# Linear ReLU attention: ten output stores moved from SyncE's queue into the loads' queue on GpSimd

## The chip, the cores and the metric

The kernel runs on one core of one Trainium2 chip. The metric is the time of one execution on the device in microseconds; lower is better. Three runs of the kernel before took 127.21, 126.92 and 126.89 us, median 126.92 us. Engines are named as in the profile: PE is TensorE, DVE is VectorE, ACT is ScalarE, POOL is GpSimd, SP is SyncE.

## The reference: attention without a softmax

```python
def reference(Q, K, V):                      # each (8, 12, 512, 64) float32
    Q_feat = np.maximum(0, Q)
    K_feat = np.maximum(0, K)
    KV = np.einsum('bhkd,bhkv->bhdv', K_feat, V)
    K_sum = np.sum(K_feat, axis=2)
    numerator = np.einsum('bhqd,bhdv->bhqv', Q_feat, KV)
    denominator = np.einsum('bhqd,bhd->bhq', Q_feat, K_sum)
    return numerator / (denominator[:, :, :, None] + 1e-10)
```

There are 96 heads of 512 rows and 64 columns. For each head a 64x64 matrix KV and a sum over K's rows are made from K and V; then every row of Q is multiplied by KV and divided by its product with that sum. Q, K and V are 12.58 MB each and so is the output: 37.75 MB are read from HBM and 12.58 MB are written to it.

## The kernel before, in words

**Tiles.** Eight heads make an octet; there are `NO` = 12 octets, 0 to 11. The heads' rows lie one after the other in HBM, so an octet is a block of 1 MB in each of Q, K, V and the output, seen as 128 partitions of 8 KB. Four heads make a group `g`; octet `o` has the groups `2*o` and `2*o + 1`. K and V are loaded by group (0.5 MB of float32 in HBM each), Q by octet (1 MB). The loads turn float32 into bfloat16 on the way, so what they write to SBUF is half of what they read: the profile counts the bytes written, and 210 GB/s of a load are 420 GB/s read from HBM. The output is float32 on both sides.

**Loads.** All loads but the first two are issued by POOL, in one queue (q0 in the profile): `load_kv` (lines 97 to 101) issues K and V of a group, `load_q` (103 to 105) Q of an octet. After `load_q(0)` a loop at line 115 issues, for each octet 1 to 11, K, V, K, V, Q: 3 MB read from HBM in five DMAs. The loop stands ahead of everything else in POOL's program; what holds an issue back is that its buffer must be free (12 buffers each for K and V, 7 for Q) and that the DMA eight places earlier in the queue must have landed, since POOL's DMAs go round eight completion semaphores. K and V of octet 0 come as float32 through the queues of SP and ACT (lines 111 and 112).

**Compute.** For each octet: `prep` and `prep_v` (DVE, ACT) apply the ReLU to K and lay K and V out for two heads at a time; `mm_kv` (PE, line 187) adds up KV and K's sums in PSUM; `evac_kv` copies them to SBUF; `qt` (lines 218 to 220) transposes Q on PE and applies the ReLU; `denom` makes the divisors and their reciprocals; `out_t` multiplies; `back` transposes the result back on PE; `norm` (line 271, DVE) divides and writes `o_sb`, twice for each octet, and then the octet's 1 MB is ready to be stored. The order on each engine is the program's order, which is written out by hand in the loops from line 321 on: the compute of octet `o` runs ahead of `backs(o - 1)`, which calls `norm` and `store`.

**Stores.** `store` (lines 277 to 287) issues one DMA of 1 MB on SP for octets 0 to 10, in a hardware queue (q1), and two of 0.5 MB for octet 11. The output tiles have `DELAY + 2` = 7 buffers. Ahead of the stores of octets 0 to 6 SP issues a small copy out of `k_sb` of octet `o + DELAY` into `scratch` (2 to 14 rows of 128 bytes, `PROBE`). This copy must wait until that K tile has landed, and since SP works through its program in order, the store behind it waits too: store 0 goes out when the first K tile of octet 5 has landed, and store 6 when that of octet 11 has. Stores 7 to 11 have no such copy, and go out when their octet is ready and SP has come to them.

Of the kernel before, what the change touches and what calls it, by code (L numbers as in the profile page):

```python
# [10 lines left out]
def kernel(  # L11
# [7 lines left out]
    nc = tc.nc  # L19
    B, H, S, D = Q.shape  # L20
# [11 lines left out]
    NO = NG // 2  # L32
    assert NO * 8 == NH and R == 16 and RQ == 32
    DELAY = 5
    PROBE = (8, 12, 4, 2, 14, 10, 6)

    fp32 = mybir.dt.float32
    bf16 = mybir.dt.bfloat16
# [3 lines left out]
    def pool(name, bufs, **kw):  # L42
        return ctx.enter_context(tc.tile_pool(name=name, bufs=bufs, **kw))

    consts = pool("consts", 1)
# [35 lines left out]
    mask = consts.tile([P, 2, 2], fp32, name="mask")  # L81
    mask8 = consts.tile([P, 4], fp32, name="mask8")
    mask8k = consts.tile([P, 2], fp32, name="mask8k")
    scratch = consts.tile([16, D], bf16, name="scratch")

    mask_h = consts.tile([P, 8, 2], fp32, name="mask_h")

# [7 lines left out]
    q_sb, k_sb, v_sb = {}, {}, {}  # L95

    def load_kv(g):
        k_sb[g] = kin.tile([P, R, D], bf16, name="k_sb")
        nc.gpsimd.dma_start(out=k_sb[g].rearrange("p r d -> p (r d)"), in_=Kr[g], single_packet=True)  # L99
        v_sb[g] = vin.tile([P, R, D], bf16, name="v_sb")  # L100
        nc.gpsimd.dma_start(out=v_sb[g].rearrange("p r d -> p (r d)"), in_=Vr[g], single_packet=True)  # L101

    def load_q(o):
        q_sb[o] = qin.tile([P, U, 2 * D], bf16, name="q_sb")
        nc.gpsimd.dma_start(out=q_sb[o].rearrange("p u f -> p (u f)"), in_=Qr[o], single_packet=True)  # L105
# [6 lines left out]
    nc.scalar.dma_start(out=v8.rearrange("p r d -> p (r d)"), in_=V8[0])  # L112
    load_q(0)
    make_identity(nc, ident)
    for o in range(1, NO):
        load_kv(2 * o)
        load_kv(2 * o + 1)
        load_q(o)

    def zero_masks():  # L120
        for h in range(NHG):
            for s in range(2):
                nc.vector.memset(mask[32 * h:32 * h + 32, 0, s:s + 1], 1.0 if h % 2 == s else 0.0)
        for t in range(2):
            nc.vector.memset(mask[:, 1, t:t + 1], 0.0)
            nc.vector.memset(mask[64 * t:64 * t + 64, 1, t:t + 1], 1.0)
# [148 lines left out]


    def store(o, o_sb):
        if o + DELAY < NO:
            n = PROBE[o]
            nc.sync.dma_start(out=scratch[0:n], in_=k_sb[2 * (o + DELAY)][0:n, 0, :])  # L280
        Ov = Or[o].rearrange("p (r d) -> p r d", d=D)
        if o == NO - 1:
            for j in range(2):
                rs = slice(RQ // 2 * j, RQ // 2 * (j + 1))
                nc.sync.dma_start(out=Ov[:, rs], in_=o_sb[:, rs])
            return
        nc.sync.dma_start(out=Ov, in_=o_sb)

    def out_tile():
        return outp.tile([P, RQ, D], fp32, name="o_sb", tag="o_sb")  # L290
# [17 lines left out]
    def backs(o):  # L308
        o_sb = out_tile()
        for j in range(2):  # L310
            norm(o, j, back(o, j), o_sb)
        store(o, o_sb)
# [26 lines left out]
    o = NO - 2  # L339
# [10 lines left out]
    o_sb = out_tile()  # L350
# [4 lines left out]
    for i in range(2):  # L355
        relu_q(o + 1, i, transp(o + 1, i), nc.vector if i == 1 else None)
    norm(o, 1, ps, o_sb)
    store(o, o_sb)
    idle(5, o + 1)
    out_t(o + 1, (0,))  # L360
# [32 lines left out]
```

## Time and profile before

| what | us |
|---|---|
| median of three runs | 126.92 |
| span of the profiled execution, first to last instruction | 125.2 |
| PE, DVE, ACT, POOL busy | 84.8, 83.4, 80.8, 32.4 |
| time of the packets of q0 (POOL's loads), as a share of 16 DMA engines' span | 74.4% |
| the same of q1 (SP: all stores, K of octet 0, the small copies) | 27.0% |

The profile gives the span of the execution that it recorded and no other time for it. The median stands 1.7 us above that span; this is what lies around the span (start and end of the program, and the difference between executions), and it is carried along unchanged below. Times inside the span are counted from its first instruction. "POOL" lines are work of GpSimd's cores, among them the writing of a DMA's descriptors; "SPq" lines are SyncE's sequencer, issuing or waiting.

### The profile page before, as it was taken

The numbers are of one execution on the slowest core, as the hardware profiler recorded it, in microseconds if no ns is written. First come the engines' busy times: TensorE is split into PE (matmuls) and PEld (weight loads), VectorE is DVE, ScalarE is ACT, GpSimd is POOL, SyncE is SP. The second block draws the span as 40 slices with busy tenths as digits, with TensorE's granted clock in tenths as the row PEclk, the third lists the DMA queues.
The fourth block names the chain that finished last, engine by engine and source line by source line (L and its number), as shares of the span: only waits on it lengthen the run. The fifth ranks groups of instructions, "written<-read, shape, count | busy, mean of one in ns | idle before, by whom it ended". The sixth has DMA issues, their size and how long they took to land.

```text
span 125.2 us, 2668 instructions
## 1 busy us (share of the span) xinstructions
PE 84.8 (68%) x1067; PEld 76.4 (61%) x1067; DVE 83.4 (67%) x192; ACT 80.8 (65%) x112; POOL 32.4 (26%) x62
## 2 busy tenths in 40 slices
PE   0005768497989898893598596199867767797800
PEld 0005548487978787791597494199766566696600
DVE  2719727979797998789148759433946936988440
ACT  0008989789898989988348688164929828637300
POOL 6903624415344241232133124034022000000000
PEclk9999999999999999999959999657999999999997
DMA  3999999999999999999999999999999999999993
GB/s 84 387 321 209 210 210 210 216 206 220 204 215 208 208 220 316 261 214 286 297 214 274 310 213 253 332 209 218 347 234 215 326 256 215 324 416 432 419 393 141
DMA packets 10348, 32.68 MB, mean 261 GB/s; under 512 B 1248, under 2 KB 1248, under 8 KB 8672
## 3 DMA queue, kind: packets, MB, share of 16 engines
q0 software_dynamic: 8064, 17.83, 74.4%
q1 hardware_dynamic: 2128, 13.64, 27.0%
q10 hardware_dynamic: 144, 1.05, 2.1%
q8 instruction: 8, 0.13, 0.4%
q14 instruction: 4, 0.03, 0.1%
HBM read 37.75 MB, written 12.58 MB: 402 GB/s over the span
## 4 chain that ended last, share of the span: by engine, by line
DMA 56%; PE 17%; DVE 15%; POOL 3%; issue 2%; ACT 1%; DVEq 1%; POOLq 0%
DMA q_sb<-in_Q_dram 25%; DMA v_sb<-in_V_dram 19%; DMA k_sb<-in_K_dram 12%; PE ps_kv L187 9%; DVE o_sb L271 8%; PE ps_bk L265 4%; PE ps_qt L208 4%; DVE kf L173 2%; DVE vo_all L175 1%; DVE vo_all L182 1%; DVEq L388 1%; POOL q_sb L105 1%; POOL v_sb L101 1%; POOL k_sb L99 1%; ACT ot_sb L240 1%
## 5 line engine op out<-in xcount | busy, mean ns | idle before, releaser
L271 DVE TENSOR_TENSOR o_sb<-ps_bk,rec 128x1024 f32<-128x1024 f32 x24 | 28.3, 1218 | 14.5 <-PE ps_bk L265 14.5
L187 PE MATMUL ps_kv<-vo_all,kf 128*128 128x132 bf16 x352 | 26.6, 237 | 6.3 <-DVE vo_all L182 5.8
L187 PEld LDWEIGHTS <-kf 128*128 128x128 bf16 x352 | 24.3, 105 | 7.5 <-issue 3.9
L208 PE MATMUL ps_qt<-ident,q_sb 128*128 128x128 bf16 x192 | 14.4, 235 | 18.6 <-DMA q_sb<-in_Q_dram 18.6
L216 ACT ACTIVATE qt<-ps_qt 128x1024 bf16<-128x1024 bf16 x23 | 22.4, 1023 | 7.0 <-PE ps_qt L208 6.8
L197 ACT CAST kvd<-ps_kv 64x260 bf16<-64x260 f32 (+1 forms) x46 | 16.6, 360 | 15.2 <-PE ps_kv L187 14.1
L240 ACT COPY ot_sb<-ps_ot 128x1024 f32<-128x1024 f32 x24 | 24.0, 1013 | 3.2 <-PE ps_ot L238 2.3
L208 PEld LDWEIGHTS <-q_sb 128*128 128x128 bf16 x192 | 12.7, 106 | 19.8 <-DMA q_sb<-in_Q_dram 19.7
L173 DVE TENSOR_SCALAR kf<-k_sb,mask 128x1024 bf16<-128x1024 bf16 x44 | 18.4, 459 | 9.1 <-DMA k_sb<-in_K_dram 9.1
L265 PE MATMUL ps_bk<-ident,ot_sb 128*128 128x128 f32 x192 | 23.4, 276 | 0.4 <-ACT ot_sb L240 0.4
L99 POOL DMA_DIRECT2D k_sb<-in_K_dram x22 | 12.6, 573 | 36.2 <-DMA q_sb<-in_Q_dram 26.7
L265 PEld LDWEIGHTS ps_bk<-ident,ot_sb 128*128 128x128 f32 x192 | 21.2, 143 | 0.7 <-ACT ot_sb L240 0.7
L238 PE MATMUL ps_ot<-qt,kvd 128*128 128x256 bf16 x96 | 13.9, 271 | 5.1 <-DVE o_sb L271 4.3
L101 POOL DMA_DIRECT2D v_sb<-in_V_dram x22 | 12.2, 553 | 18.7 <-DMA k_sb<-in_K_dram 12.3
L238 PEld LDWEIGHTS <-kvd 128*128 128x128 bf16 x96 | 8.9, 97 | 7.8 <-issue 5.8
L175 DVE TENSOR_SCALAR vo_all<-v_sb,mask 128x1024 bf16<-128x1024 bf16 x22 | 10.7, 484 | 1.6 <-DMA v_sb<-in_V_dram 1.6
L180 ACT ACTIVATE vo_all<-v_sb,mask 128x1024 bf16<-128x1024 bf16 x10 | 11.5, 1153 | 0.2
L247 PEld LDWEIGHTS <-qt 128*128 128x128 bf16 x192 | 6.8, 96 | 4.8 <-ACT qt L216 2.0
L247 PE MATMUL ps_den<-kvd,qt 128*128 128x16 bf16 x192 | 7.3, 179 | 3.0 <-ACT kvd L167 1.7
L105 POOL DMA_DIRECT2D q_sb<-in_Q_dram x12 | 7.1, 595 | 7.9 <-DMA v_sb<-in_V_dram 4.1
L156 ACT ACT_TABLE_LOAD x1 | 1.3, 1283 | 9.8 <-DMA v_first<-in_V_dram 9.8
L182 DVE TENSOR_SCALAR vo_all<-v_sb,mask 128x1024 bf16<-128x1024 bf16 x12 | 5.7, 478 | 0.0
(32 smaller groups left out, 42.9 us busy)
## 6 DMA issues: line engine op xcount, KB each, us to landing
out_dram<-o_sb SPq DMA_DIRECT2D x11, 1024.0 KB, 8.6
q_sb<-in_Q_dram POOLq DMA_DIRECT2D x12, 512.0 KB, 14.7
k_sb<-in_K_dram POOLq DMA_DIRECT2D x22, 256.0 KB, 14.2
v_sb<-in_V_dram POOLq DMA_DIRECT2D x22, 256.0 KB, 13.3
v_first<-in_V_dram ACTq DMA_DIRECT2D x1, 1024.0 KB, 9.0
k_first<-in_K_dram SPq DMA_DIRECT2D x1, 1024.0 KB
out_dram<-o_sb SPq DMA_DIRECT2D x2, 512.0 KB, 3.7
scratch<-k_sb SPq DMA_DIRECT2D x1, 1.0 KB
```

The costliest lines, as they stand in the source:

```text
L99: nc.gpsimd.dma_start(out=k_sb[g].rearrange("p r d -> p (r d)"), in_=Kr[g], single_packet=True)
L101: nc.gpsimd.dma_start(out=v_sb[g].rearrange("p r d -> p (r d)"), in_=Vr[g], single_packet=True)
L173: nc.vector.tensor_scalar(kf[g][:, :, s, :], k_sb[g], scalar1=0.0, scalar2=mask[:, 0, s:s + 1], op0=Alu.max, op1=Alu.mult)
L187: nc.tensor.matmul(ps_kv[:, g % 2, 0:2 * (D + 2)].rearrange("p (t d) -> p t d", t=2), kf[g][:, r, :, :].rearrange("p s d -> p (s d)"), vo[ ...
L197: copy(kvd[o % NK][64 * c:64 * c + 64, 4 * gs.start + s:4 * gs.stop:2, c * D1:c * D1 + D1].rearrange("p (g t) d -> p g t d", t=2), ps_kv[6 ...
L208: nc.tensor.transpose(ps[:, u, :], q_sb[o][:, i * (U // 2) + u, :], ident)
L216: nc.scalar.activation(to, ps, Act.Relu)
L238: nc.tensor.matmul(ps[:, i], kvd[o % NK][:, h, 1:2 * D + 1], q[:, :, h, :], start=True, stop=True, skip_group_check=True)
L240: nc.scalar.copy(ot[o][:, :, 4 * j:4 * j + 4], ps.rearrange("p h u c -> p u h c"))
L247: nc.tensor.matmul(ps[:, u], qt_sb[o % NZ][:, u, :], kvd[o % NK][:, :, 0:2 * D1:2 * D1 - 1], start=True, stop=True, skip_group_check=True)
L265: nc.tensor.transpose(ps[:, 2 * v:2 * v + 2].rearrange("p c d -> p (c d)"), ot[o][:, 8 * j + v].rearrange("p h c -> p (h c)"), ident32)
L271: nc.vector.tensor_tensor(o_sb[:, rs], ps, rec[o][:, rs].unsqueeze(2).to_broadcast([P, 16, D]), op=Alu.mult)
```

## The change

The seven small copies, `PROBE` and the tile `scratch` are gone. The stores of octets 0 to 9 are issued by POOL in the queue of the loads; those of octets 10 and 11 stay on SP. POOL's loop of loads stops at octet 5, and the loads of octet `o + 6` are issued right behind the store of octet `o`, from within `store`. POOL's program is then: Q of octet 0, the loads of octets 1 to 5, store 0, loads 6, store 1, loads 7, and so on to store 5, loads 11, and then stores 6, 7, 8 and 9.

```diff
-    PROBE = (8, 12, 4, 2, 14, 10, 6)
...
-    scratch = consts.tile([16, D], bf16, name="scratch")
...
-    for o in range(1, NO):
+
+    def load_octet(o):
         load_kv(2 * o)
         load_kv(2 * o + 1)
         load_q(o)
+
+    for o in range(1, DELAY + 1):
+        load_octet(o)
...
     def store(o, o_sb):
-        if o + DELAY < NO:
-            n = PROBE[o]
-            nc.sync.dma_start(out=scratch[0:n], in_=k_sb[2 * (o + DELAY)][0:n, 0, :])
         Ov = Or[o].rearrange("p (r d) -> p r d", d=D)
         if o == NO - 1:
             for j in range(2):
                 rs = slice(RQ // 2 * j, RQ // 2 * (j + 1))
                 nc.sync.dma_start(out=Ov[:, rs], in_=o_sb[:, rs])
             return
-        nc.sync.dma_start(out=Ov, in_=o_sb)
+        if o >= NO - 2:
+            nc.sync.dma_start(out=Ov, in_=o_sb)
+            return
+        nc.gpsimd.dma_start(out=Ov, in_=o_sb, single_packet=True)
+        if o + DELAY + 1 < NO:
+            load_octet(o + DELAY + 1)
```

`single_packet=True` is the option that the loads carry already.

## The prediction

> **What bounds the kernel now.** I read the page's slices first, then its DMA queues and its chain, then the DMA issues of POOL and SP in order of time, and last tables by stage.
>
> ```profile
> DMA  3999999999999999999999999999999999999993
> GB/s 84 387 321 209 210 210 210 216 206 220 204 215 208 208 220 316 261 214 286 297 214 274 310 213 253 332 209 218 347 234 215 326 256 215 324 416 432 419 393 141
> ...
> q0 software_dynamic: 8064, 17.83, 74.4%
> q1 hardware_dynamic: 2128, 13.64, 27.0%
> ...
> DMA 56%; PE 17%; DVE 15%; POOL 3%; issue 2%; ACT 1%; DVEq 1%; POOLq 0%
> ```
>
> The DMA engines are busy in every slice but the first and the last, and no compute engine is. Loads count half of what they read: the slices at 204 to 220 GB/s are 408 to 440 GB/s of HBM reads, and the slices at 416 to 432 near the end are stores alone. So the same ceiling holds throughout, and the time is the bytes divided by it plus a start and an end. Next, the stage tables (the last columns are DMA share and GB/s written):
>
> ```profile
> 47.00:52.00 5.00, 3.99 (x55) 3.35 (x54) 4.38 (x8) 4.65 (x8) 1.01 (x2) 1.00 1.04 309
> ...
> 113.00:119.00 6.00, 4.76 (x51) 3.71 (x48) 4.24 (x7) 3.05 (x3) 0.00 (x0) 1.00 1.02 429
> ...
> 112.00:119.00 7.00, 5.76 (x68) 4.69 (x65) 4.53 (x9) 3.58 (x5) 0.00 (x0) 1.00 1.02 425
> 119.00:121.00 2.00, 0.00 (x0) 0.00 (x0) 1.42 (x2) 0.00 (x0) 0.00 (x0) 1.00 0.91 379
> 121.00:125.20 4.20, 0.00 (x0) 0.00 (x0) 0.00 (x0) 0.00 (x0) 0.00 (x0) 0.80 0.51 208
> ```
>
> The first row is a store and loads together; the next two are stores alone, at 425 to 429; the last two are the run-out. And the issues, POOL's first:
>
> ```profile
> 10.99 0.76 POOL L99 DMA_DIRECT2D k_sb<-in_K_dram  x1 [4.84 <-DMA q_sb<-in_Q_dram]
> ...
> 27.23 0.53 POOL L99 DMA_DIRECT2D k_sb<-in_K_dram  x1 [2.96 <-DMA q_sb<-in_Q_dram]
> ...
> 38.46 0.53 POOL L99 DMA_DIRECT2D k_sb<-in_K_dram  x1 [0.69 <-DMA k_sb<-in_K_dram]
> ...
> 42.23 0.53 POOL L99 DMA_DIRECT2D k_sb<-in_K_dram  x1 [1.98 <-DMA q_sb<-in_Q_dram]
> ...
> 61.21 0.53 POOL L99 DMA_DIRECT2D k_sb<-in_K_dram  x1 [3.23 <-DMA q_sb<-in_Q_dram]
> ...
> 86.16 0.53 POOL L99 DMA_DIRECT2D k_sb<-in_K_dram  x1 [0.69 <-issue]
> ...
> 91.18 0.66 POOL L99 DMA_DIRECT2D k_sb<-in_K_dram  x1 [3.24 <-DMA q_sb<-in_Q_dram]
> ...
> 94.93 0.53 POOL L105 DMA_DIRECT2D q_sb<-in_Q_dram  x1 [0.77 <-DMA v_sb<-in_V_dram]
> ```
>
> ```profile
> SPq L280 <- DMA k_sb<-in_K_dram: 71.5, 7, 42.0
> ```
>
> ```profile
> 103.95 11.58 SPq L287 DMA_DIRECT2D out_dram<-o_sb  x5
> 119.32 1.46 SPq L285 DMA_DIRECT2D out_dram<-o_sb  x2
> ```
>
> ```profile
> 26.23 2.36 DVE L271 TENSOR_TENSOR o_sb<-ps_bk,rec 128x1024 f32<-128x1024 f32 x2 [0.89 <-PE ps_bk L265]
> ...
> 66.20 2.35 DVE L271 TENSOR_TENSOR o_sb<-ps_bk,rec 128x1024 f32<-128x1024 f32 x2 [1.25 <-PE ps_bk L265]
> ...
> 104.27 2.36 DVE L271 TENSOR_TENSOR o_sb<-ps_bk,rec 128x1024 f32<-128x1024 f32 x2 [2.97 <-PE ps_bk L265]
> ```
>
> At 10.99 POOL issues its ninth load after 4.84 us of waiting for the first to land: at most eight are out. From there each issue follows a landing, so the issues' period is the DMA's pace: (42.23 - 27.23) / 2 = 7.50 us for an octet's loads alone, (91.18 - 61.21) / 3 = 9.99 us for an octet's loads with a store beside them. The SP line is the small copies' wait, which holds the stores back on purpose.
>
> **The change part by part.**
>
> *Seven copies and ten stores leave SP.* The copies' 2 to 14 rows of 128 bytes are nothing beside a 1 MB store, and SP has nothing behind them but stores. Gain 0 by themselves.
>
> *Ten stores are issued by POOL.* An issue of a load takes 0.53 us there; ten are 5.3 us, in an engine that waits 36.2 + 18.7 + 7.9 = 62.8 us ahead of its loads. The trace shows no issue of a store on POOL: from below I bound it by that 0.53 us, from above by twice it, 1.06 us, for a row of 8 KB written instead of 2 or 4. With six DMAs to an octet that is 6 x 0.53 to 6 x 1.06 = 3.2 to 6.4 us of POOL in every 10 us: hidden either way. I take 0.
>
> *POOL now waits for an octet's result, and the next loads stand behind that wait.* This is the new wait that could hurt: a late `norm(o)` holds up all loads from octet o + 6 on. POOL comes to store 0 when it issued the first K tile of octet 6 before, 38.46, and `norm(0)` ends at 26.23 + 2.36 = 28.6: 9.9 us of room. Store 5 comes at about 86.2, and `norm(5)` ends at 68.6: 17.6 us. Behind stores 6 to 9 there are no loads; store 9 waits for the `norm` that ends at 106.6, when the loads of octet 11 and three stores are still in the queue. Cost 0. If that cover went, loads would be late by what is missing.
>
> *Each store counts among the eight DMAs that may be out.* Six DMAs for 10 us instead of five: eight hold 13.3 us of transfers, so the queue doesn't run dry. Cost 0.
>
> *The store's bytes move one after the other with the loads', not beside them.* Before, a store costs 9.99 - 7.50 = 2.49 us of the DMA's time. Alone, 1.0486 MB cost 2.47 us at 425 GB/s and 2.44 at 429. In the shared queue the price is unknown. One end is the store-only price, 2.44; the other is the loads' own pace, a third of 7.50 for 1 MB, 2.50. I take the middle of the store-only rows, 2.455, because they are the same bytes in the same direction, one behind the other in one queue: 6 x (2.49 - 2.455) = 0.2 us of gain for stores 0 to 5; stores 6 to 11 ran alone before but for the first, and gain nothing. At the loads' pace ten stores give 6 x 0.01 + 4 x 0.045 = 0.2 us of loss. The Trainium skill ("DMA: Bandwidth & Descriptors", section "Issuing engines are not separate DMA queues") says that all issuers' transfers run on the same 16 engines, and that another issuer saves issue time only; by that the sum here would be 0 and the time 126.9. Rows and rule are within what can be told apart.
>
> *Q lands earlier.* While a store moves (47 to 52 us), 309 GB/s are written: with 420 in all, x of loads and 420 - x of stores, 420 - x/2 = 309 gives x = 222, so loads go at half pace, and it is mostly Q that is in the queue. Now Q of an octet goes ahead of the store, some 1.5 to 2.5 us sooner; K and V come when they did. That helps compute, which isn't what is short. It is worth 0 while the stores' bytes set the end.
>
> *The end.* Before, the last store is issued at 120.45 and needs 3.7 us (the median of its group). After, one store less stands ahead of the last Q, and six follow, of 2.46 us each: the same bytes. Cost 0.
>
> Sum: 0.2 us off a span of 125.2, so 125.0; with the 1.7 us around it, 126.7 against the median of 126.92. Here 0.3% (0.38 us) is about what a measurement can tell from no change.
>
> **The rivals.**
>
> *A gap at each store (slower).* Before, an engine that ends a packet of one queue has one of the other queue ready. In one queue each engine must go from a load (HBM to SBUF, with a cast) to a store and back, and could stand still at the turn. Nearest row: when the stores' queue ran short at 119 to 121, 379 instead of 425 GB/s moved, 2 x (1 - 379/425) = 0.22 us lost at a fresh start. Ten stores at half of that are 1.1 us (127.8), at all of it 2.2 us (128.9). It decides from (0.38 + 0.2) / 10 = 0.06 us a store. [...] Against it: the two queues mixed now, with 13.64 MB of q1 in 2128 packets, turn far more often, and that costs only 2.49 against 2.455. The Trainium skill (same page, section "Specifications") puts the first byte of a DMA from GpSimd at about 1 us against 0.6 from SP; exposed ten times that would be an estimate of 10 us more, but no row here shows such a start exposed, since a load lands 14 us after its issue.
>
> *The run-out shrinks (faster).* From 121 on, 208 x 4.2 = 0.87 MB move, 2.0 us at 425; some 1.4 us of the 4.2 are a store's completion and the end of the program, so 0.75 us of DMA time is idle there, and 0.22 us before. The chain from 80.8 us on is compute, released by a Q tile; if that Q and the last ones land 1.5 us sooner, so do the last stores, and up to 0.9 us of idle time goes: 125.8 to 126.5, about 126.2. Against it: 16 engines end unevenly, and one that is behind sets the end whenever the stores are issued.
>
> *POOL's wait holds loads up.* 127.3 or more; the 9.9 us of room speak against it.
>
> **How the numbers follow.** Main case, bytes as before with 0.2 us less or more: 0.50, 126.4 to 127.1, of which 0.14 lies under 126.54. Run-out: 0.20. Gap: 0.28. POOL's wait: 0.02. So faster 0.14 + 0.20 = 0.34, same 0.36, slower 0.30. The range 126.0 to 128.0 leaves out the far end of the run-out (0.06) and of the gap (0.12); the main case's own range is 126.4 to 127.1.
>
> **What would show it.** Right: DMA busy in every slice as now; POOL's issue period still near 9.95 us in the middle; SP with three DMAs at the end and no waits before; store-to-landing times of 12 us or so, since they queue behind loads; no idle time of POOL that `norm` ends. Wrong towards slower: slices below 9 in the DMA row or a period above 10.1; POOL waiting for L271; a long landing of the last stores. Wrong towards faster: the last `norm` ending over 1 us before 120.4 and a shorter tail behind it.

## The result: a small gain, at the edge of what can be measured

The changed kernel took 126.38 us (median of 126.21, 126.33, 126.42 and 126.50) against 126.91 us before: a ratio of 0.9951, 95% interval 0.9939 to 0.9962, 0.5 us less. Measured a second time, beside other kernels, it took 126.62 us (twelve executions, 126.22 to 127.28) against 126.84: 0.9987, 0.9972 to 1.0002. So the gain is 0.2 to 0.5 us, and it comes with a wider spread: 1.06 us among those twelve executions, 0.37 us among the 31 of the kernel before that stood beside them (126.62 to 126.99). The ratios are formed from executions measured beside each other, without those over 1.5% above their kernel's fastest, so they can differ from the quotient of the two medians, by up to 0.6%.

The page's slices, queues and chain of the changed kernel:

```profile
DMA  3999999999999999999999999999999999999992
GB/s 95 397 310 205 216 205 210 215 206 215 206 214 210 210 216 358 229 216 333 257 213 291 299 210 256 335 210 234 354 220 217 352 233 218 323 426 415 429 410 121
...
q0 software_dynamic: 9504, 28.32, 94.9%
q1 hardware_dynamic: 576, 3.15, 6.3%
...
DVE 34%; DMA 27%; PE 24%; ACT 6%; issue 4%; DVEq 1%; ACTq 0%
```

The DMA engines are as full as before, now with ten stores in q0. The chain of waits has moved from DMA (56% before) to compute (27% DMA), but that is a trap: the chain follows whatever came later at each step, by however little. The experiment without store 9 below shows what really sets the end. The same stages as before, by windows:

```profile
47.00:52.00 5.00, 4.47 (x62) 4.08 (x60) 4.05 (x8) 4.42 (x8) 1.06 (x2) 1.00 1.05 314
112.00:119.00 7.00, 4.80 (x51) 3.74 (x49) 5.20 (x8) 3.07 (x4) 0.00 (x0) 1.00 1.00 421
113.00:119.00 6.00, 4.26 (x46) 3.51 (x46) 4.29 (x7) 2.09 (x3) 0.00 (x0) 1.00 1.00 422
119.00:121.00 2.00, 0.00 (x0) 0.00 (x0) 0.46 (x1) 0.00 (x0) 0.00 (x0) 1.00 1.00 416
121.00:124.70 3.70, 0.00 (x0) 0.00 (x0) 0.00 (x0) 0.00 (x0) 0.00 (x0) 0.75 0.39 161
```

The dip at 119 to 121 is gone (416 instead of 379 GB/s). POOL's DMA issues in order of time:

```profile
53.39 0.53 POOL L97 DMA_DIRECT2D k_sb<-in_K_dram  x1 [0.28 <-DMA k_sb<-in_K_dram]
...
57.44 0.54 POOL L289 DMA_DIRECT2D out_dram<-o_sb  x1 [0.73 <-DVE o_sb L273]
...
93.07 0.53 POOL L97 DMA_DIRECT2D k_sb<-in_K_dram  x1 [0.42 <-DMA k_sb<-in_K_dram]
...
97.12 0.54 POOL L289 DMA_DIRECT2D out_dram<-o_sb  x1 [0.73 <-DVE den L257]
...
105.95 0.61 POOL L289 DMA_DIRECT2D out_dram<-o_sb  x1 [3.35 <-DVE o_sb L273]
```

An octet with its store now takes (93.07 - 53.39) / 4 = 9.92 us, against 9.99 before. An issue of a store costs POOL 0.54 us. The only long wait for a `norm` is that of store 9, with no loads behind it. SP's waits and issues, and the last `norm` of DVE:

```profile
SPq L287 <- DVE o_sb L273: 113.1, 1, 113.1
```

```profile
114.23 0.34 SPq L287 DMA_DIRECT2D out_dram<-o_sb  x1
118.36 1.46 SPq L284 DMA_DIRECT2D out_dram<-o_sb  x2
```

```profile
103.30 2.36 DVE L273 TENSOR_TENSOR o_sb<-ps_bk,rec 128x1024 f32<-128x1024 f32 x2 [4.58 <-PE ps_bk L267]
...
117.10 2.35 DVE L273 TENSOR_TENSOR o_sb<-ps_bk,rec 128x1024 f32<-128x1024 f32 x2 [1.64 <-PE ps_bk L267]
```

```profile
out_dram<-o_sb POOLq DMA_DIRECT2D x10, 1024.0 KB, 14.3
q_sb<-in_Q_dram POOLq DMA_DIRECT2D x12, 512.0 KB, 13.1
...
out_dram<-o_sb SPq DMA_DIRECT2D x2, 512.0 KB, 4.2
```

The last `norm` ends 1.0 us sooner than before (119.5 against 120.4), and the last stores take 4.2 us to land instead of 3.7: half of the lead of compute is given back to the queue.

### The profile page after: what moved, and what is told of

It reads as the page before. It is cut to its first block, busy times and chain, and to the rows that moved or that the text cites. A ratio compares the mean times of both kernels' runs of the same rounds, so it can differ in the third digit from the quotient of the medians.

```text
span 124.7 us, 2642 instructions
## 1 busy us (share of the span) xinstructions
PE 86.4 (69%) x1067; PEld 77.5 (62%) x1067; DVE 83.1 (67%) x192; ACT 80.8 (65%) x112; POOL 38.1 (31%) x72
## 4 chain that ended last, share of the span: by engine, by line
DVE 34%; DMA 27%; PE 24%; ACT 6%; issue 4%; DVEq 1%; ACTq 0%
DVE o_sb L273 15%; DMA q_sb<-in_Q_dram 11%; DMA v_sb<-in_V_dram 9%; PE ps_kv L189 8%; PE ps_bk L267 7%; DMA v_first<-in_V_dram 7%; DVE kf L175 5%; PE ps_kv L165 5%; DVE vo_all L177 3%; PE ps_qt L210 3%; DVE vo_all L184 3%; DVE den L257 2%; DVE rec L261 2%; DVE own L252 2%; ACT vo_all L158 2%
## 5 line engine op out<-in xcount | busy, mean ns | idle before, releaser
L189 PEld LDWEIGHTS <-kf 128*128 128x128 bf16 x352 | 23.8, 104 | 7.9 <-issue 4.2
L242 ACT COPY ot_sb<-ps_ot 128x1024 f32<-128x1024 f32 x24 | 24.1, 1012 | 5.3 <-PE ps_ot L240 4.4
L210 PE MATMUL ps_qt<-ident,q_sb 128*128 128x128 bf16 x192 | 15.2, 242 | 13.6 <-DMA q_sb<-in_Q_dram 13.6
L210 PEld LDWEIGHTS <-q_sb 128*128 128x128 bf16 x192 | 13.6, 110 | 14.5 <-DMA q_sb<-in_Q_dram 14.4
L97 POOL DMA_DIRECT2D k_sb<-in_K_dram x22 | 13.2, 602 | 25.3 <-DMA q_sb<-in_Q_dram 21.1
L177 DVE TENSOR_SCALAR vo_all<-v_sb,mask 128x1024 bf16<-128x1024 bf16 x22 | 10.6, 482 | 1.1 <-DMA v_sb<-in_V_dram 1.1
L289 POOL DMA_DIRECT2D out_dram<-o_sb x10 | 5.4, 544 | 13.7 <-DVE o_sb L273 4.8
## 6 DMA issues: line engine op xcount, KB each, us to landing
out_dram<-o_sb POOLq DMA_DIRECT2D x10, 1024.0 KB, 14.3
```

Of the source, the lines that this page charges most:

```text
L177: nc.vector.tensor_scalar(vo[g % NB][:, :, 0, 2:D + 2], v_sb[g], scalar1=mask[:, 1, 0:1], scalar2=None, op0=Alu.mult)
L189: nc.tensor.matmul(ps_kv[:, g % 2, 0:2 * (D + 2)].rearrange("p (t d) -> p t d", t=2), kf[g][:, r, :, :].rearrange("p s d -> p (s d)"), vo[ ...
L210: nc.tensor.transpose(ps[:, u, :], q_sb[o][:, i * (U // 2) + u, :], ident)
L242: nc.scalar.copy(ot[o][:, :, 4 * j:4 * j + 4], ps.rearrange("p h u c -> p u h c"))
```

## The experiments

**What is read from them.** Totals differ by tenths of a microsecond, so the pace in the middle is read too. The trace records when each of the 16 DMA engines reports its share of a DMA as done. The table takes these reports for the V tile of the last group of octet 5 and for that of octet 11, six octets later: the time between them over six, for the first engine to report and for the mean of the 16, and how far the last engine is behind the first at octet 11 (its lag). Loads alone run at about 7.50 us an octet by the mean, in every trace where they do run alone. The last column is the time of the very execution that the trace shows. The experiments were measured in four sessions on different chips, each beside the kernel before, whose median was 126.84 to 126.98 us; between sessions the ratios are compared, and microseconds within one alone.

| kernel | us an octet, first | mean | lag | this execution |
|---|---|---|---|---|
| before | 10.01 | 10.07 | 1.61 | not recorded |
| before, stores with the option | 9.99 | 10.08 | 2.02 | 127.04 |
| before, no copies, no delay | 9.99 | 10.06 | 1.82 | 132.01 |
| changed | 9.92 | 10.00 | 2.05 | 126.42 |
| changed, second time | 9.93 | 10.01 | 2.26 | 126.80 |
| changed, copies put back | 9.95 | 10.03 | 2.47 | 127.19 |
| changed, 28 copies | 10.01 | 10.06 | 1.97 | 127.34 |
| changed, no option | 9.93 | 10.00 | 2.48 | 127.28 |
| changed, stores in pairs | 9.93 | 10.04 | 3.07 | 127.51 |
| changed, half stores | 9.97 | 10.09 | 2.51 | 127.49 |
| changed, quarter stores | 9.98 | 10.08 | 1.96 | 130.27 |
| changed, store 10 on GpSimd | 9.93 | 10.01 | 2.82 | 127.86 |
| changed, without store 9 | 9.92 | 10.00 | 2.35 | 124.07 |
| changed, store 9 on SP | 9.95 | 10.00 | 1.80 | 126.52 |

The theories: **M**, stores that move beside loads in a second queue cost DMA time, and one queue saves it; **C**, the small copies cost it. A third question is whether the stores' bytes or compute set the end.

### The copies put back into the changed kernel

```diff
     def store(o, o_sb):
+        if o + DELAY < NO:
+            n = PROBE[o]
+            nc.sync.dma_start(out=scratch[0:n], in_=k_sb[2 * (o + DELAY)][0:n, 0, :])
```

> The changed kernel with the seven small copies on SyncE put back (no store stands behind them; stores stay in the loads' queue). Theory M, mixing: what the change gains is that stores no longer move beside loads in a second queue; the copies cost nothing, so 126.4 and a landing period of 9.90 us for an octet with its store, as in the changed kernel. Theory C, copies: the gain is that the copies' packets and completions are gone; then most of the 0.5 us comes back, 126.7 to 126.9, period 9.96 to 10.00.

Measured: 126.68 us against 126.98, ratio 0.998 (0.9969 to 0.9991). That is between the theories' numbers, and it stands between the changed kernel's own two ratios. The pace is 9.95 and 10.03 us by the first and the mean engine, near the changed kernel's 9.92 to 9.93 and 10.00 to 10.01 and not at 10.01 and 10.07; the last engine's landings, of which the expectation spoke, came at 10.05, spoilt by a stall at 62.7 (below). The four long packets of that stall took 2.98 us instead of 0.69, which is 0.02 us an octet for the mean engine: all that its 10.03 has over 10.00 to 10.01. So most of the gain is not the copies'; a tenth of a microsecond may be.

### The kernel before without copies, stores as soon as they are ready

```diff
     def store(o, o_sb):
-        if o + DELAY < NO:
-            n = PROBE[o]
-            nc.sync.dma_start(out=scratch[0:n], in_=k_sb[2 * (o + DELAY)][0:n, 0, :])
```

> The kernel before without its small copies: all stores stay on SyncE and go as soon as their octet is ready, beside the loads from the second octet on. Read from the pace, not from the total. Theory M: an octet's loads with a store beside them still land every 9.99 us or a little more. Theory C: every 9.90 us. In both the total is worse, since about three more stores go ahead of the last loads (3 x 2.46 us) while the compute behind the last Q, 13 us to the end before, stays: 129 to 133 us. If the total stays near 126.9, the delay of the stores was worth nothing.

Measured: 132.07 us, ratio 1.0422 (1.0389 to 1.0455). POOL's issues, and the last windows:

```profile
53.49 0.53 POOL L99 DMA_DIRECT2D k_sb<-in_K_dram  x1 [0.33 <-issue]
...
93.63 0.53 POOL L99 DMA_DIRECT2D k_sb<-in_K_dram  x1 [0.97 <-DVE o_sb L271]
```

```profile
112.00:118.00 6.00, 4.40 (x54) 3.96 (x51) 5.47 (x13) 3.30 (x8) 0.00 (x0) 1.00 1.03 283
118.00:124.00 6.00, 4.96 (x61) 4.13 (x62) 3.31 (x6) 3.29 (x4) 0.00 (x0) 1.00 0.40 165
124.00:130.20 6.20, 0.92 (x9) 0.68 (x7) 2.36 (x2) 0.00 (x0) 0.00 (x0) 0.80 0.50 200
```

The pace is (93.63 - 53.49) / 4 = 10.03 us an octet, 9.99 by the first engine and 10.06 by the mean: that of the kernel before, with no copies in it. This is M. The copies account for 10.07 - 10.06, some 0.01 us an octet, or for nothing: this stretch holds four of the eight instruction packets described below and the kernel before has five in its own, which is 0.01 us an octet as well. The total shows what the delay of the stores is worth: the last loads land 7.6 us later (114.5 against 106.9 us for the last V tile), and then the DMA engines have too little to do while compute finishes (shares 0.40 and 0.50).

### Four times as many copies

```diff
     def store(o, o_sb):
+        if o + DELAY < NO:
+            for j in range(4):
+                nc.sync.dma_start(out=scratch[:, j], in_=k_sb[2 * (o + DELAY)][0:16, j, :])
```

> The changed kernel with 28 small copies on SyncE, four of 16 rows where the kernel before had one of 2 to 14 rows. Theory C, the copies cost by themselves: put back once they left the kernel at 0.998 instead of 0.995, so they cost about 0.3 us; four times as many and on all 16 engines cost 1.2 us or more, 127.6 and over. Theory M, side by side: 28 x (34 + 15) ns of packets on each engine are 1.4 us if they add to the loads, and nothing if they fall into what the engines have over while they wait for data; then 126.4 to 126.7, and the 0.3 us seen was the slowest engine's lag in that run. The pace of the middle tells the two apart: above 10.0 us an octet with C, 9.90 to 9.93 with the second.

Measured: 127.21 us, ratio 1.0033 (1.0021 to 1.0046), 0.6 us above the changed kernel beside it (126.62). The pace is 10.01 and 10.06: 0.05 us by the mean for four copies of 16 rows, 0.013 us a copy; by the first engine (0.09) and by the total (0.6 us for 28) it is 0.02. So a copy has a price, less than half of the 0.05 us that the expectation counts for its packet and its completion (34 and 15 ns; in this trace they took 19 and 14 ns on average), and the seven small ones, of 2 to 14 rows, cost some 0.1 us. The lag explains nothing here (1.97 us).

### Stores in quarters, between the loads

```diff
-        nc.gpsimd.dma_start(out=Ov, in_=o_sb, single_packet=True)
-        if o + DELAY + 1 < NO:
-            load_octet(o + DELAY + 1)
+        def quarter(j):
+            rs = slice(RQ // 4 * j, RQ // 4 * (j + 1))
+            nc.gpsimd.dma_start(out=Ov[:, rs], in_=o_sb[:, rs], single_packet=True)
+        n = o + DELAY + 1
+        for j in range(4):
+            quarter(j)
+            if n < NO:
+                load_half(2 * n + j // 2, j % 2)   # K, V, K, V
+        if n < NO:
+            load_q(n)
```

> The changed kernel with each of the ten stores on GpSimd cut into four quarters by columns, and in the middle one quarter ahead of each of the four K and V loads: one queue as in the changed kernel, but reads and writes of HBM alternate four times as often. Theory M1, two queues served in turn by the engines cost the time: the middle keeps 9.90 us an octet, 126.4. Theory M2, reads and writes of HBM at close quarters cost it, in one queue or in two: the middle goes back to 9.95 to 10.00 and the total to 126.6 to 126.9. The quarters' own price (rows of 2 KB instead of 8) is read from stores 6 to 9, which run alone: 2.45 us per MB in the changed kernel; what they take over that is to be taken off the middle too.

Measured: 129.84 us, ratio 1.0166. The total was mistaken in both theories, for a reason of its own:

```profile
POOL 6903533324335353662552653563553553670000
...
DMA  4999999999999999999999999999999999999940
```

The DMA engines are idle in the last slice, and the program isn't over. The last landing is at 124.8 us; what the program waits for is POOL's last instruction, a drain, which ends at 127.7 us (next experiment). The pace answers the question: 9.98 by the first engine, of which the quarters' own price must be taken off. Eight quarters in a row ran alone in 5.06 us by the first engine, 2.53 us per MB, 0.08 above whole stores; 9.98 - 0.08 = 9.90. In this trace four times as many changes between reading and writing, in one queue, cost nothing in the pace: that speaks for the second queue as what costs (M1), and against the changes. It is one trace, and in two queues the engines may change more often still.

### Store 10 on GpSimd too

```diff
-        if o >= NO - 2:
+        if o >= NO - 1:
             nc.sync.dma_start(out=Ov, in_=o_sb)
```

> The changed kernel with the store of octet 10 on GpSimd too, so that only the last octet's two halves are on SyncE. By the bytes alone nothing changes: 126.4. But in the changed kernel's trace GpSimd's last instruction before the end, a drain, lasts from its last issue (105.9) to 122.5, that is 2.7 us past the landing of its last store (119.74), and in the kernel with quarters it ended 2.8 us after SyncE was done and so set the end. Here its last store lands at about 121.3 to 122.5, so the drain ends at 124.0 to 125.2 where SyncE is done at 123.8: 126.6 to 127.8.

Measured: 126.83 us, ratio 0.9997 (0.9987 to 1.0008), 0.2 us above the changed kernel beside it. In the trace POOL's drain ends at 125.30, 2.8 us after the last landing in its queue (122.52) and 0.6 us after SyncE had seen the last store land (124.69). So the stores at the very end belong on SyncE: a store on GpSimd must land 2.7 us ahead of the others in order not to be the end. In the changed kernel the drain ended at 122.5, with 1.3 us to spare.

### Without the store of octet 9

```diff
     def store(o, o_sb):
+        if o == NO - 3:
+            return
```

> The changed kernel without the store of octet 9, so that octet's output is left out: 1 MB less in the run-out, loads untouched. If the stores' bytes alone set the end (as the prediction's main case says), the end comes up to 2.45 us earlier, until compute is reached: the last store is issued at 119.5 and takes about 0.75 us to its first byte, 1.3 us of transfer and 0.35 us of completion, so 121.9 instead of 123.7: about 1.8 us, 124.6. If compute set the end (the rival of the shrinking run-out), 126.3 to 126.4.

Measured: 124.25 us, ratio 0.9789 (0.9764 to 0.9814): 2.1 to 2.6 us below the changed kernel (126.98 x 0.9951 = 126.36 or x 0.9987 = 126.81), for a store of 2.45 us. The whole of it came off, as far as that spread tells, so the stores' bytes set the end. The trace shows on which engine: the first one reports the last half store 2.6 us after its issue with store 9 and without it (119.48 to 122.10, 117.95 to 120.56 us), so it waits for that issue, which means for compute, in both; the last one reports at 123.74 and at 121.40, and it is the last that carries the end. The expected floor of 121.9 us by compute was too high, since the last store was issued at 117.95 here and not at 119.5; compute's own end moves by that much between executions. No run here makes DVE's work shorter; but where 1 MB less of stores takes off its whole time, the 34% that the chain of waits put on DVE are no measure of what a saving on DVE would bring.

### Whole packets in the kernel before

```diff
-        nc.sync.dma_start(out=Ov, in_=o_sb)
+        nc.sync.dma_start(out=Ov, in_=o_sb, single_packet=True)
```

> The kernel before with the loads' option single_packet on its stores from SyncE, which stay in their own queue beside the loads. Theory M with a price for each switch between queues: the engines change queue an eighth as often, so an octet with a store comes down from 9.99 to about 9.92 us and the total to 126.4 to 126.6. If the price is that of two queues being worked on at all, or if the option does nothing for SyncE's stores, 9.99 us and 126.9.

Measured: 126.90 us, ratio 1.0006 (0.9997 to 1.0014), pace 9.99 and 10.08: no change. The trace has the same 2128 packets in q1, and nothing in it shows whether SyncE's queue heeds the option. That the price is one for each switch is neither shown nor excluded.

### Stores on GpSimd without the option

```diff
-        nc.gpsimd.dma_start(out=Ov, in_=o_sb, single_packet=True)
+        nc.gpsimd.dma_start(out=Ov, in_=o_sb)
```

> The changed kernel without single_packet on its ten stores. In one queue there is nothing to switch to for most of the time, so the packets' size should not matter: pace 9.91 us, 126.4 to 126.6. If the option is what makes the store cost 2.42 us instead of 2.50, the pace goes to 9.99 and the time to 126.9.

Measured: 126.70 us, ratio 0.9987 (0.9971 to 1.0002), the same ratio as the changed kernel's second measurement, pace 9.93 and 10.00. No effect of the option shows here. Its trace shows a long execution, 127.28 us, and some 0.1 us of that is POOL's drain, which ended at 124.73 when SyncE had been done at 124.62.

### The changed kernel again, and where its spread comes from

> The changed kernel once more, beside the next three: 0.994 to 0.996 of the kernel before. The profiled execution shows how much of its end differs between executions: the pace of the middle (an octet with its store every 9.90 us) should repeat to 0.02 us, the lag of the slowest DMA engine behind the fastest (2.0 us in the changed kernel's profile, 1.7 in that of before, 2.5 in the one with the copies put back) need not.

Measured: 126.62 us, ratio 0.9987 (0.9972 to 1.0002); the 0.994 to 0.996 expected was missed: the upper edge of the interval reaches no change. The pace repeats to 0.01 us, the lag does not. In the last column of the table the executions with one queue and whole stores order themselves by it, nearly (28 copies and store 10 on GpSimd, which have a cost of their own, left aside): lags of 1.80, 2.05, 2.26, 2.47 and 2.48 us go with 126.52, 126.42, 126.80, 127.19 and 127.28 us. The last of the 16 engines sets the end, and each falls behind by what hits it alone.

Two things hit single engines. One is in every trace: eight packets of 16 KB of another queue, about 0.95 us each, one at a time. The page lists them:

```profile
q8 instruction: 8, 0.13, 0.4%
```

In the trace of before the first of them, with 1.18 us at 24.1, takes the lag from 0.41 to 1.72 us, and it stays there to the end; the later ones hit engines that were ahead. The other is in the traces of the changed order alone: load packets that take 0.4 to 1.2 us instead of 0.17, on one engine or several at once, just behind a store: at 62.7 with the copies put back, at 72.4 in the changed kernel's second trace (lag from 1.55 to 2.25), at 82.3 with store 10 on GpSimd, at 92.6 without store 9, at 62.5 to 62.9 with pairs. The changed kernel's first trace has none, nor have the trace without the option, whose lag grew to 2.48 us all the same, and the three with the stores on SyncE. The stalls account for the differences in the mean pace among the kernels with whole stores in one queue: what their packets took over 0.17 us, shared among 16 engines and six octets, is 0.01 us an octet in the second trace and with store 10 on GpSimd (10.01 each), 0.02 with the copies put back (10.03) and 0.03 with pairs (10.04); without it all of them stand at 10.00 to 10.01. In one queue nothing evens such a delay out: on each engine everything that follows is late by the same amount (in the second trace the lag stays at 2.2 to 2.3 us from 73 to 115 us).

### Pairs and halves: is it the turn from a store to a load?

```diff
# pairs: after the loads of octets 1 to 6
+  stores 0, 1 | loads 7, 8 | stores 2, 3 | loads 9, 10 | stores 4, 5 | loads 11 | stores 6 to 9
# halves: stores 0 to 5, n = o + DELAY + 1
+        for j in range(2):
+            rs = slice(RQ // 2 * j, RQ // 2 * (j + 1))
+            nc.gpsimd.dma_start(out=Ov[:, rs], in_=o_sb[:, rs], single_packet=True)
+            load_kv(2 * n + j)
+        load_q(n)
```

> The changed kernel with stores 0 to 5 in pairs: the loads of octets 1 to 6, stores 0 and 1, loads 7 and 8, stores 2 and 3, loads 9 and 10, stores 4 and 5, loads 11, then stores 6 to 9 as before. The same bytes in one queue with three turns from a store to a load instead of six. If turning costs nothing (theory M alone), the pace stays 9.91 us an octet and the time is that of the changed kernel, 126.4 to 126.6. If the packets of 0.4 to 1.2 us that stood just behind a store in four of the changed order's traces (62.7, 72.4, 82.3 and 92.6 us) belong to the turn, half as many turns bring the median 0.1 to 0.2 us down and shorten the upper end of the times (127.28).

> The changed kernel with stores 0 to 5 cut into halves by columns, each half ahead of one K and V pair of octet o + 6: store runs of 0.5 MB between loads instead of 1 MB (2 MB in the kernel with pairs); stores 6 to 9 stay whole. Theory S, a long run of writes now and then holds up the reads right behind it: pairs had five load packets of 0.46 to 0.73 us behind a store and times of 126.41 to 128.41 us, whole stores 126.22 to 127.28, quarters had none; so halves end at 126.8 or below in all executions, with a median of 126.4 to 126.5 (rows of 4 KB cost 2.48 us per MB as the last two halves did, 0.2 us in all) and no such packets in the trace. If the stalls come with the turns, of which there are twice as many, the median is 126.8 or more and the upper end above 127.3.

Measured: pairs 127.21 us (126.41 to 128.41), ratio 1.0015 (0.9998 to 1.0033); halves 127.75 us (126.60 to 128.52), ratio 1.0057 (1.0033 to 1.0081). Fewer turns with longer runs of writes came out worse (pairs stand 0.5 us above the kernel without the option, measured in the same session, and their interval just touches that of the changed kernel's second measurement), and more turns with shorter runs are worse clearly; the expectations of both kernels miss. By the mean pace, 10.04 and 10.09 us, half or all of what the single queue saves is gone in these two traces. The halves' trace has four packets of 0.75 to 1.17 us at 55.4 to 56.0 and single ones behind later stores; the quarters' trace has only short ones (0.81 us at most) and a lag of 1.96. Long packets of this kind were seen only where stores and loads follow one another in one queue, with whole, paired, half and quarter stores, though not in every trace; what sets them off, and why the whole stores suffer least in the median, stays open.

### Store 9 on SyncE

```diff
-        if o >= NO - 2:
+        if o >= NO - 3:
             nc.sync.dma_start(out=Ov, in_=o_sb)
```

> The changed kernel with store 9 on SyncE too, ahead of stores 10 and 11. Store 9 then moves beside stores 6 to 8 and the last loads (0.1 us more by theory M), and the last landing in GpSimd's queue comes 2.4 us sooner, so that its drain ends at about 120 instead of 122.5 to 124.2 and cannot set the end. If the drain sets the end in the longer executions of the changed kernel, its upper end (127.28) falls to 126.9; if not, the times are those of the changed kernel or 0.1 us above, 126.4 to 126.7.

Measured: 126.52 us, ratio 0.9964 (0.9952 to 0.9976), five executions of 126.22 to 126.77. The step about the drain was wrong: store 9 moved beside stores 6 to 8 and delayed them, and the drain ended at 123.45, later than the changed kernel's 122.48. The time lies between the changed kernel's two ratios, and its trace has no stall. No version here is shown to beat the changed kernel.

## Why the prediction was right or wrong, step by step

The forecast was 126.7 us, 126.0 to 128.0, most likely no change that can be told; measured were 126.38 and 126.62. The direction and the mechanism hold, though the second measurement's interval reaches no change; one term of the sum was too small.

- *What bounds the kernel.* Right. DMA is full in all slices, and a store less at the end takes 2.1 to 2.6 us off.
- *Copies at 0.* Nearly: 0.01 to 0.02 us a copy of 16 rows by the 28 copies, some 0.1 us for the seven.
- *POOL's issues, bracketed at 0.53 to 1.06 us.* 0.54 us, at the lower end, and hidden, as said.
- *POOL's wait for `norm`.* Right: only store 9 waits long (3.35 us), with no loads behind it.
- *Eight DMAs out are enough.* Right: no slice below 9 in the middle. The stores' time to land was 14.3 us, not the 12 told.
- *The store's price in the shared queue.* This is the term that was mis-sized. The step took 2.49 - 2.455 = 0.035 us a store, 0.2 us in all. By the mean engine an octet gained 10.07 - 10.00 = 0.07 to 0.08 us, 0.46 us for six, of which the copies are some 0.1; so a store beside loads costs some 0.06 us more than one behind them, nearly twice the step's value. The row that it was taken from, POOL's issue period, rounds what each engine shows: it follows the last engine's landing and carries its lag along. The rule of the Trainium skill ("DMA: Bandwidth & Descriptors", section "Issuing engines are not separate DMA queues"), that another issuer saves issue time only, does not hold to this precision: 10.06 against 10.00 us an octet by the mean engine, with no copies in either, is a cost of the second queue. The step's two levels were both too low by this measure: a store costs 10.07 - 7.50 = 2.57 us beside the loads, not 2.49, and 10.00 - 7.50 = 2.50 behind them, the end of the bracket at the loads' own pace and not 2.455. The 0.2 us of loss foreseen for that end did not come because the price before was higher too; that the sum's 0.2 us lies so near the 0.2 to 0.5 measured is in part luck.
- *The end at 0.* Right in the sum, but the end is the last engine's, and what it had lost on the way (the lag) varies by 0.5 to 1 us between executions. The prediction named engines that end unevenly, and only as an argument against the faster rival.
- *The gap at each store.* Not at each store: the paces exclude the 0.06 us from which it would have decided. But stalls behind a store do come in some executions, on a few engines. Whether they separate the second ratio from the first is not shown: the second trace has them (lag from 1.55 to 2.25 us), but the trace without the option reached 127.28 us with none, and the two ratios come from four and from twelve executions.
- *The run-out shrinks.* Compute's lead came (1.0 us), and the dip at 119 to 121 went; the last store landed 0.4 us sooner (123.74 against 124.15), since it is the last engine that lands it, 1.6 us behind the first. The chance of 0.20 was right to be small.

## What to carry to other kernels

Where DMA is full from start to end, look at each of its engines: the last one sets the end, and a delay that hits one engine alone is never made up while all of them carry the same bytes. Putting stores behind loads in one queue saves the price of a second queue, here some 0.06 us per MB stored beside loads, and needs no copies to hold the stores back; but it leaves the time open to stalls behind a store, so judge such a change by many executions and by the pace of the middle, not by one median. Keep the last stores off GpSimd's queue.

## What the runs showed of the hardware that was not expected

- GpSimd's drain at the program's end ended 2.7 to 2.8 us after the last landing of a DMA of its queue (122.48 against 119.74 us in the changed kernel, 125.30 against 122.52 with store 10 there), and 4.0 us with quarters (127.68 against 123.72). With the loads last, as in the kernel before, it was 2.3 us (113.25 against 110.93).
- Eight packets of 16 KB of an instruction queue, 0.9 to 1.2 us each, each hold up one DMA engine; the first of them, at 24 to 26 us, raised the lag by 0.5 to 1.3 us in the 14 traces (0.41 to 1.72 in that of before), and it was not made up.
- Rows of 2 KB written from SBUF to HBM (the quarter stores) cost 2.53 us per MB against 2.45 for rows of 8 KB, by the first engine, in one queue and with no loads beside them.
- A 16-row copy of 128 bytes a row cost the loads beside it 0.01 to 0.02 us.
